# Three float32r matmuls over split operands become one plain float32 matmul

## The chip, the core and the metric

The kernel runs on one core of a Trainium2 chip. The metric is device time in microseconds (us), the median of three runs. Engines are named as the profile names them: PE is TensorE (matmuls), PEld its loads of stationary operands, DVE is VectorE, ACT ScalarE, POOL GpSimd, SP the engine that issues transfers.

## What is computed

Two layers of a hybrid block on 256 context tokens and 1024 latent tokens, width 1024, all in float32. Each layer normalises its input, modulates it, multiplies it by a wide input projection, runs four groups of heads (latent attention, global attention, windowed attention with sinks, a two-way state-space scan), and puts the gated results through one output projection with a residual.

```
h = rmsnorm(x, norm_w) * (1 + scale[:, None]) + shift[:, None]
hc = rmsnorm(xc, norm_w) * (1 + scale_c) + shift_c
pl = split_cols(h @ w_in, IN_WIDTHS)
pc = split_cols(hc @ w_in, IN_WIDTHS)
...
x = x + gate[:, None] * (jnp.concatenate([ya_l, yb_l, yc_l, yd_l], axis=-1) @ w_out)
if need_ctx_out:
    xc = xc + gate_c * (jnp.concatenate([ya_c, yb_c, yc_c, yd_c], axis=-1) @ w_out)
```

The second layer needs no context output, so its output projection covers the 8 latent tiles of 128 tokens, the first layer's all 10.

## The kernel before

**Products.** A number is kept as a pair: its rounding to float32r (hi) and the rest (lo). `mm3` (lines 127 to 130) makes a product of three matmuls, hi by hi, lo by hi and hi by lo, into one PSUM bank. It serves the input projection (`products` at line 618, 128 weight columns by up to 512 tokens, and the token-major part at line 1011, 128 tokens by 256 columns), the up-projections of the latent attention (lines 853 to 892) and the output projection (line 1377). Each contracts 1024 features in 8 steps of 128, the up-projections 128 or 256.

**Splitting.** `split_w` (line 284) loads weights into the ring `bg`, has ACT round them into one slot and DVE or POOL subtract into a second. `make_ht` (line 385) does the same with the modulated input, `third` (line 773) with queries and keys, `prep` of the output projection (line 1349) with the attention outputs. The normalised latent vectors go to DRAM as pairs (`d_c`, line 825) and come back for the up-projections (line 842).

**Attention.** For each pair of heads and each group of 512 or 256 queries, `main` (line 1196) goes over blocks of 128 keys: scores of both heads (lines 1214 to 1222), exponentials on ACT, and then, one block late, the products of probabilities and values (line 1230), which are plain float32 matmuls: the two heads write the two halves of the PSUM partitions. Row maxima of later queries are found meanwhile (`maxima`, line 1127, single float32r matmuls, DVE reduces them); minus the maximum enters the scores through one further row of the operands. In the latent branch the scores are three matmuls; in the other two branches, whose heads have 64 features, hi and lo stand on top of each other in 128 rows, and two matmuls do (lines 1219 and 1222).

**Scan.** `chunk_a` (line 522) sums decays over tokens with a triangular matrix of ones; its moving operand is split as well, so four matmuls (line 540).

**Order.** The work is written down in one order, in which scan steps, up-projections, maxima and the loads of the next weights are spread between the products of the input projection and between the blocks of attention; each engine then keeps its own queue in the order in which its instructions come out. Slots of 4 KB per partition (35 of them) are handed out and returned in program order, PSUM is divided by tags (`MX` 3 banks, `S2` 3, `ACC` 1, `TR` 2). Weight chunks are fetched one ahead of their use.

## Time and profile before

| | |
|---|---|
| median of 3 runs | 1937.92 us (1937.03 to 1938.29) |
| span of the profiled execution | 1922.1 us |
| PE busy | 1839.9 us, 9658 records |
| weight loads busy | 1327.6 us |
| DVE, ACT, POOL busy | 1128.8, 751.5, 772.8 us |
| moved by DMA | 231.52 MB |

The profile is of one execution; the span goes from its first instruction to its last. A record is what the hardware ran: a matmul of the program can leave one or two. Matmuls overlap, since the next starts while the last one drains, so the sum or the mean of their times is more than what they occupy; the distance between two starts says that. A few per cent of the records can be missing. The stages in time are roughly: preparation to 50 us, first input projection with the scan to 555, first attention to 910, first output projection to 1050, then the same for the second layer to 1460, 1810 and the end.

### The profile page before, as it was taken

The numbers are of one execution on the slowest core, as the hardware profiler recorded it, in microseconds if no ns is written. First come the engines' busy times: TensorE is split into PE (matmuls) and PEld (weight loads), VectorE is DVE, ScalarE is ACT, GpSimd is POOL, SyncE is SP. The second block draws the span as 40 slices with busy tenths as digits, with TensorE's granted clock in tenths as the row PEclk, the third lists the DMA queues.
The fourth block names the chain that finished last, engine by engine and source line by source line (L and its number), as shares of the span: only waits on it lengthen the run. The fifth ranks groups of instructions, "written<-read, shape, count | busy, mean of one in ns | idle before, by whom it ended". The sixth has DMA issues, their size and how long they took to land. (4 is left out here: it accounts for less than half of the span.)

```text
span 1922.1 us, 27855 instructions
## 1 busy us (share of the span) xinstructions
PE 1839.9 (96%) x9658; PEld 1327.6 (69%) x9658; DVE 1128.8 (59%) x2290; ACT 751.5 (39%) x2060; POOL 772.8 (40%) x735
## 2 busy tenths in 40 slices
PE   6999999999999999999999999999999999999898
PEld 4767888899854455555787778878986445555586
DVE  6867864464365555447546678745645456444854
ACT  5423433332314445445423333333321444544541
POOL 1313541143316666545223125522241566654522
PEclk9999999999999999999899999999999999999899
DMA  8464323265763233122511433232766422310421
GB/s 293 136 225 143 121 83 126 92 195 174 213 175 88 76 98 76 50 61 91 175 57 39 149 112 128 92 116 81 253 200 189 121 81 80 80 36 10 135 115 55
DMA packets 130396, 231.52 MB, mean 120 GB/s; under 512 B 13784, under 2 KB 74560, under 8 KB 130256
## 3 DMA queue, kind: packets, MB, share of 16 engines
q1 hardware_dynamic: 130256, 229.75, 38.1%
q8 instruction: 76, 1.25, 0.3%
q14 instruction: 64, 0.52, 0.1%
HBM read 161.15 MB, written 68.44 MB: 119 GB/s over the span
## 5 line engine op out<-in xcount | busy, mean ns | idle before, releaser
L1146 DVE TENSOR_REDUCE mp<-ps_s 128x1 f32<-128x512 f32 (+3 forms) x428 | 267.3, 659 | 246.3 <-PE ps_s L1142 206.8
L1242 POOL TENSOR_TENSOR ac<-ac,P 128x512 f32<-128x512 f32 (+3 forms) x248 | 301.2, 1226 | 212.9 <-ACT P L1223 185.2
L1223 ACT ACTIVATE P<-ps_st 128x512 f32<-128x512 f32 (+3 forms) x456 | 239.7, 553 | 269.7 <-PE ps_st L1222 127.7
L128 PE MATMUL ps_fm<-hh,wfm_hi 128*128 128x512 f32 x576 | 237.7, 413 | 2.8 <-DVE kb L658 2.1
L130 PE MATMUL ps_fm<-hl,wfm_hi 128*128 128x512 f32 x576 | 232.0, 403 | 2.6 <-POOL hl L403 2.3
L129 PE MATMUL ps_fm<-hh,wfm_lo 128*128 128x512 f32 x576 | 231.6, 402 | 0.0
L128 PE MATMUL ps_tm<-wtm_hi,hh 128*128 128x256 f32 x512 | 146.6, 286 | 0.9 <-DVE qkhl L783 0.9
L129 PE MATMUL ps_tm<-wtm_hi,hl 128*128 128x256 f32 x512 | 145.6, 284 | 0.0
L130 PE MATMUL ps_tm<-wtm_lo,hh 128*128 128x256 f32 x512 | 145.3, 284 | 0.0
L128 PEld LDWEIGHTS ps_fm<-hh,wfm_hi 128*128 128x128 f32 x576 | 110.0, 191 | 32.2 <-issue 8.7
L130 PEld LDWEIGHTS ps_fm<-hl,wfm_hi 128*128 128x128 f32 x576 | 110.0, 191 | 28.7 <-POOL hl L403 5.3
L1236 POOL TENSOR_TENSOR ac<-P 128x1024 f32<-128x1024 f32 (+1 forms) x30 | 65.5, 2184 | 143.5 <-ACT P L1223 138.8
L129 PEld LDWEIGHTS ps_fm<-hh,wfm_lo 128*128 128x128 f32 x576 | 109.9, 191 | 18.8 <-issue 1.1
L128 PE MATMUL ps_o<-wo_hi,yh 128*128 128x512 f32 x288 | 113.9, 396 | 0.4 <-ACT yh L1353 0.4
L129 PE MATMUL ps_o<-wo_hi,yl 128*128 128x512 f32 x288 | 113.2, 393 | 0.1
L130 PE MATMUL ps_o<-wo_lo,yh 128*128 128x512 f32 x288 | 112.9, 392 | 0.0
L1230 PE MATMUL ps_acc<-P,vt 128*64 128x512 f32 (+3 forms) x416 | 101.4, 540 | 0.5 <-ACT P L1223 0.5
L128 PEld LDWEIGHTS ps_tm<-wtm_hi,hh 128*128 128x128 f32 x512 | 98.2, 192 | 2.9 <-DVE qkhl L783 1.2
L130 PEld LDWEIGHTS ps_tm<-wtm_lo,hh 128*128 128x128 f32 x512 | 98.3, 192 | 0.8 <-issue 0.4
L129 PEld LDWEIGHTS ps_tm<-wtm_hi,hl 128*128 128x128 f32 x512 | 98.3, 192 | 0.4
L1380 POOL TENSOR_TENSOR xres<-xres,dl 128x512 f32<-128x512 f32 x32 | 41.8, 1305 | 112.3 <-DVE dl L1379 112.3
L1219 PE MATMUL ps_st<-qq,kk 128*128 128x512 f32 (+3 forms) x208 | 84.1, 404 | 0.0
(345 smaller groups left out, 4169.7 us busy)
## 6 DMA issues: line engine op xcount, KB each, us to landing
wfm_raw<-in_w_fm_dram SPq DMA_DIRECT2D x36, 512.0 KB
wm<-in_w_mod_dram SPq DMA_DIRECT2D x64, 256.0 KB
d_q<-qkhl SPq DMA_DIRECT2D x18, 512.0 KB
wm<-in_w_mod_dram SPq DMA_DIRECT2D x16, 512.0 KB
d_gate<-th SPq DMA_DIRECT2D x32, 256.0 KB
wtm_raw<-in_w_tm_dram SPq DMA_DIRECT2D x16, 512.0 KB
qq<-d_q SPq DMA_DIRECT2D x32, 256.0 KB
wo_raw<-in_w_out_dram SPq DMA_DIRECT2D x16, 512.0 KB
```

The source lines that it names most:

```text
L128: mm(o, lhsT=lh, rhs=rh, start=first, stop=False)
L129: mm(o, lhsT=ll, rhs=rh, start=False, stop=False)
L130: return mm(o, lhsT=lh, rhs=rl, start=False, stop=last)
L1146: nc.vector.tensor_reduce(out=dst, in_=p[:, :nu * w].rearrange("p (u k) -> p u k", u=nu), axis=AX.X, op=ALU.max)
L1219: mm(st, lhsT=k(k0, 128), rhs=q(q0, 128), start=True, stop=False)
L1223: nc.scalar.activation(out=pts[:, h, :w], in_=st, func=AF.Exp, scale=op["scale"])
L1230: mm(acc[h * 64:h * 64 + 64, c0:c0 + w], lhsT=op["v"].tile(kb)[:, v0:v0 + 64], rhs=pts[:, h, :w], start=(bi == 0), stop=(bi == len(blocks) ...
L1236: nc.gpsimd.tensor_tensor(out=s[:, :, :n], in0=sums[0][:, :, :n], in1=pts[:, :, :n], op=ALU.add)
L1242: eng.tensor_tensor(out=s[:, h, c0:c0 + w], in0=s[:, h, c0:c0 + w], in1=pts[:, h, :w], op=ALU.add)
L1380: (nc.vector if t == ts[-1] else nc.gpsimd).tensor_tensor(out=xt.t[:, js], in0=xt.t[:, js], in1=d, op=ALU.add)
```

## The change

`mm3` becomes `mm1`, one matmul on float32 operands. All pairs are gone: weights land in a slot directly (`load_w`), the modulated input is written once, queries, keys and up-projected operands are kept once in DRAM, the normalised latent vectors stay in SBUF. The scores of every branch are one matmul over `kd + 1` rows (97 or 65). The decay sums take two matmuls, one per direction, over unsplit operands. The maxima stay float32r and read the float32 operands under that type; in the two branches with 64 features they read one row more, which holds zeros then. Comments and docstrings are dropped.

```diff
-    def mm3(o, lh, ll, rh, rl, first, last):
-        mm(o, lhsT=lh, rhs=rh, start=first, stop=False)
-        mm(o, lhsT=ll, rhs=rh, start=False, stop=False)
-        return mm(o, lhsT=lh, rhs=rl, start=False, stop=last)
+    def mm1(o, l, r, first, last):
+        return mm(o, lhsT=l, rhs=r, start=first, stop=last)
...
-    def split_w(src, name, n=1024, eng=None):
-        raw = bg((P, n), name=name + "_raw")
-        nc.sync.dma_start(out=raw, in_=src)
-        hi = Slot([P, n], F32R, name + "_hi")
-        lo = Slot([P, n], F32R, name + "_lo")
-        nc.scalar.copy(hi.t, raw)
-        (eng or nc.vector).tensor_tensor(out=lo.t, in0=raw, in1=f32(hi.t), op=ALU.subtract)
-        return hi, lo
...
+    def load_w(src, name):
+        w = Slot([P, 1024], F32, name)
+        nc.sync.dma_start(out=w.t, in_=src)
+        return w
...
-                nc.scalar.activation(out=hf[:, :n], in_=src, func=AF.Identity, scale=sc, bias=bi)
-            hi = hh[k](lo, n)
-            nc.vector.tensor_copy(hi, hf[:, :n])
-            eng = nc.gpsimd if k % 2 else nc.vector
-            eng.tensor_tensor(out=hl[k](lo, n), in0=hf[:, :n], in1=f32(hi), op=ALU.subtract)
+                nc.scalar.activation(out=h[k](lo, n), in_=src, func=AF.Identity, scale=sc, bias=bi)
...
                 for d in range(2):
-                    for e in range(2):
-                        mm(pseg[:, 0:256], lhsT=st_r[d], rhs=ta[:, d, e, :], start=(d == 0 and e == 0), stop=(d == 1 and e == 1))
+                    mm(pseg[:, 0:256], lhsT=st_f[d], rhs=ta[:, d, :], start=d == 0, stop=d == 1)
...
-            r = mm3(p, hi.t[:, c], lo_.t[:, c], hh[k](lo, n), hl[k](lo, n), k == 0, k == 7)
+            r = mm1(p, w[0].t[:, k * P:(k + 1) * P], h[k](lo, n), k == 0, k == 7)
...
-                mm3(p[:, :n], wh, wl, *W["ck", lo], True, True)
...
+                mm1(p[:, :n], W["k"].t[:, pair * P:pair * P + P], res["ckv"](lo, n), True, True)
...
-                    if br == 0:
-                        k0, k1 = op["k"][h]
-                        mm(st, lhsT=k(k0, 96), rhs=q(q0, 96), start=True, stop=False)
-                        mm(st, lhsT=k(k1, 96), rhs=q(q0, 96), start=False, stop=False)
-                        mm(st, lhsT=k(k0, 97), rhs=q(q1, 97), start=False, stop=True)
-                    else:
-                        k0, k1 = op["k"][0]
-                        mm(st, lhsT=k(k0, 128), rhs=q(q0, 128), start=True, stop=False)
-                        if mo is not None:
-                            mm(st, lhsT=ident_r, rhs=mask_r[:, mo:mo + w], start=False, stop=False)
-                        mm(st, lhsT=k(k1, 65), rhs=q(q1, 65), start=False, stop=True)
+                    mm(st, lhsT=op["k"][h].tile(kb, 0, kd + 1), rhs=op["q"][h](lo + c0, w, 0, kd + 1), start=True, stop=mo is None)
+                    if mo is not None:
+                        mm(st, lhsT=ident_r, rhs=mask_r[:, mo:mo + w], start=False, stop=True)
...
-                    mm3(p, yh[:, k, :], yl[:, k, :], wo[k][0].t[:, js], wo[k][1].t[:, js], k == 0, k == 7)
+                    mm1(p, y[k].tile(t), wo[k].t[:, js], k == 0, k == 7)
```

Two places show how the order of PE's instructions moves. The first is in the input projection of the first layer, where scan steps (`ps_y`, `ps_yt`, `ps_seg`, `ps_cb`) stand between the products (`ps_fm`). PE before:

```order
L128 MATMUL ps_fm<-hh_441,wfm_hi 128x512
L129 MATMUL ps_fm<-hh_441,wfm_lo 128x512
L558 MATMUL ps_y<-ssd_cx,EW 128x64 x2
L561 MATMUL ps_y<-st_cx,ssd_cx 128x128 x2
L578 MATMUL ps_yt<-con,yy 128x128
L540 MATMUL ps_seg<-TA,mask_r 128x256 x2
L130 MATMUL ps_fm<-hl_446,wfm_hi 128x512
L128 MATMUL ps_fm<-hh_442,wfm_hi 128x512
L129 MATMUL ps_fm<-hh_442,wfm_lo 128x512
L130 MATMUL ps_fm<-hl_447,wfm_hi 128x512
```

PE in the changed kernel, at the like place:

```order
L125 MATMUL ps_fm<-h_544,wfm 128x512
L125 MATMUL ps_fm<-h_545,wfm 128x512
L125 MATMUL ps_fm<-h_546,wfm 128x512
L536 MATMUL ps_y<-xt,EW 128x64 x2
L539 MATMUL ps_y<-st,cf 128x128 x2
L518 MATMUL ps_seg<-TA,mask_r 128x256
L525 MATMUL ps_cb<-cf,bf 128x128
L518 MATMUL ps_seg<-TA,mask_r 128x256
L556 MATMUL ps_yt<-con,yy 128x128
L125 MATMUL ps_fm<-h_428,wfm 128x512
```

Each product is one instruction in place of three, and the scan's steps, which are as many as before, stand between whole products.

The second place is in the global attention of the first layer (`ps_st` scores, `ps_acc` values, `ps_s` maxima, `ps_m` their transpose). PE before:

```order
L1142 MATMUL ps_s<-kk_cx 128x256 x4
L1219 MATMUL ps_st<-qq_5595,kk 128x512
L1222 MATMUL ps_st<-ql_5597,k_5594 128x512
L1219 MATMUL ps_st<-qq_5596,kk 128x512
L1222 MATMUL ps_st<-ql_5598,k_5594 128x512
L1230 MATMUL ps_acc<-P,vt 64x512 x2
L1219 MATMUL ps_st<-qq_5595,kk 128x512
```

PE in the changed kernel:

```order
L1062 MATMUL ps_s<-k_cx 128x256 x4
L1129 MATMUL ps_st<-q_3664,k 128x512
L1129 MATMUL ps_st<-q_3665,k 128x512
L1090 MATMUL ps_m<-con,mt 4x128
L1139 MATMUL ps_acc<-P,vt 64x512 x2
L1129 MATMUL ps_st<-q_3664,k 128x512
```

Two score matmuls per key block stand where four stood; the maxima and the values keep their number and their place.

## Rows read from the trace of the kernel before

**Rows 1.** The page, its line of busy time: share of the span, instructions.

```profile
PE 1839.9 (96%) x9658; PEld 1327.6 (69%) x9658; DVE 1128.8 (59%) x2290; ACT 751.5 (39%) x2060; POOL 772.8 (40%) x735
```

**Rows 2.** By stage: length, busy PE, PEld, DVE, ACT, POOL, PEclk, DMA, GB/s.

```profile
0.00:50.00 50.00, 33.14 (x209) 22.97 (x209) 31.18 (x81) 27.78 (x69) 10.26 (x18) 0.93 0.84 287
50.00:555.00 505.00, 484.99 (x3107) 409.69 (x3107) 309.09 (x688) 165.95 (x411) 159.93 (x189) 0.99 0.47 152
555.00:910.00 355.00, 351.53 (x1504) 186.80 (x1503) 198.05 (x341) 171.68 (x509) 201.78 (x156) 0.98 0.30 82
910.00:1050.00 140.00, 135.54 (x617) 108.81 (x617) 76.61 (x170) 54.70 (x178) 42.69 (x38) 0.96 0.28 97
1050.00:1460.00 410.00, 390.22 (x2396) 340.27 (x2395) 259.47 (x556) 142.21 (x342) 139.64 (x165) 0.98 0.44 143
1460.00:1810.00 350.00, 344.43 (x1388) 180.10 (x1388) 193.69 (x324) 152.62 (x415) 187.94 (x141) 0.98 0.30 81
1810.00:1922.10 112.10, 100.00 (x447) 78.96 (x443) 60.71 (x136) 36.52 (x140) 30.55 (x29) 0.96 0.26 95
```

**Rows 3.** The chain that ended last, in second attention: start us, us, piece.

```profile
1512.92 1.01 PE ps_acc L1230 x4
1513.93 0.43 PE ps_s L1142
1514.36 0.43 PE ps_st L1219
1514.79 0.23 PE ps_st L1222
...
1518.86 1.87 PE ps_acc L1230 x8
```

**Rows 4.** Timeline of PE, first output projection: start us, us, instruction.

```profile
964.83 0.39 PE L128 MATMUL ps_o<-wo_hi,yh 128*128 128x512 f32 x1
...
966.19 0.39 PE L128 MATMUL ps_o<-wo_hi,yh 128*128 128x512 f32 x1
```

**Rows 5.** Timeline of PE, second input projection.

```profile
1359.74 0.28 PE L130 MATMUL ps_tm<-wtm_lo,hh 128*128 128x256 f32 x1
...
1361.18 0.28 PE L130 MATMUL ps_tm<-wtm_lo,hh 128*128 128x256 f32 x1
```

**Rows 6.** Timeline of PE, scan steps within the first input projection.

```profile
223.16 0.66 PE L561 MATMUL ps_y<-st,cf 128*128 128x128 f32 x4
223.66 0.27 PE L578 MATMUL ps_yt<-con,yy 128*128 128x128 f32 x1
```

**Rows 7.** Groups of PE instructions, shapes apart: count, busy us, mean ns, idle before.

```profile
L128 PE MATMUL ps_fm<-hh,wfm_hi 128*128 128x512 f32 x576 | 237.7, 413 | 2.8 <-DVE kb L658 2.1 <-ACT hf L399 0.3 <-DVE hh L401 0.2
...
L128 PE MATMUL ps_tm<-wtm_hi,hh 128*128 128x256 f32 x512 | 146.6, 286 | 0.9 <-DVE qkhl L783 0.9
...
L128 PE MATMUL ps_o<-wo_hi,yh 128*128 128x512 f32 x288 | 113.9, 396 | 0.4 <-ACT yh L1353 0.4
...
L1219 PE MATMUL ps_st<-qq,kk 128*128 128x512 f32 x128 | 57.6, 450 | 0.0
L128 PE MATMUL ps_fm<-hh_cx,wfm_hi 128*128 128x256 f32 x192 | 56.9, 296 | 0.0
...
L1214 PE MATMUL ps_st<-qh,kh 96*128 96x512 f32 x128 | 52.0, 406 | 0.1
...
L128 PE MATMUL ps_tm<-wtm_hi,hh_cx 128*128 128x256 f32 x96 | 28.1, 293 | 2.2 <-DVE rb L732 2.2
...
L540 PE MATMUL ps_seg<-TA,mask_r 128*128 128x256 f32 x144 | 27.5, 302 | 2.0 <-DVE TA L518 1.7
L1219 PE MATMUL ps_st<-qq,kk_cx 128*128 128x512 f32 x64 | 27.2, 445 | 0.3 <-DVE th L668 0.3
...
L1214 PE MATMUL ps_st<-qh,kh_cx 96*128 96x512 f32 x32 | 13.5, 422 | 0.0
```

**Rows 8.** Groups of PE instructions, shapes together, score line 1219.

```profile
L1219 PE MATMUL ps_st<-qq,kk 128*128 128x512 f32 (+3 forms) x208 | 84.1, 404 | 0.0
```

More of the change, by code (lines that the diff above doesn't have):

```diff
@@ L361, in alloc_ht @@
     def alloc_ht(half):
-        hh, s1 = toks([f"hh{4 * half + k}" for k in range(4)], F32R)
-        hl, s2 = toks([f"hl{4 * half + k}" for k in range(4)], F32R)
-        return hh, hl, s1 + s2
+        return toks([f"h{4 * half + k}" for k in range(4)], F32)
     def transposed(xs, lo, n, k):
@@ L613, in fetch @@
             br, half = j[1]
-            return [split_w(w_tm[L, br, half, :, u, :], f"wtm{u}", eng=nc.gpsimd if (br * 2 + half, u) in POOL_TM else None)
-                    for u in range(2)]
-        return [split_w(w_fm[L, j[1]], "wfm", eng=nc.gpsimd if j[1] in POOL_FM else None)]
+            return [load_w(w_tm[L, br, half, :, u, :], f"wtm{u}") for u in range(2)]
+        return [load_w(w_fm[L, j[1]], "wfm")]
     def products(ht, w, lo, n, tag="MX", each=lambda: None, ks=range(8), p=None):
-        hh, hl, _ = ht
-        hi, lo_ = w[0]
+        h = ht[0]
         if p is None:
@@ L814, in start_ssd, with norm @@
                 todo.extend(ssd.steps(g))
-        def norm(keys, nfeat, groups, col, c0, done):
+        def norm(keys, nfeat, groups, col, done):
             srcs = [res[k] for k in keys]
@@ L955, in in_proj @@
         conv_fin(jobs[1][3], xp, True)
-        for u in both[0] + both[1]:
-            free_all(u)
+        free_all(both[0] + both[1])
         for ji, j in enumerate(jobs):
@@ L1042, in ones_row @@
             for lo, n in ((0, NCTX), (NCTX, NLAT)):
-                nc.vector.tensor_copy(tok(lo, n, row, row + 1), ones[row:row + 1, 0:1].to_broadcast([1, n]))
+                nc.vector.tensor_copy(f32r(tok(lo, n, row, row + 1)), ones[row:row + 1, 0:1].to_broadcast([1, n]))
         def rows(tok, p0, src, with_ctx=True):
@@ L1101, in begin @@
[L1101 to L1119 removed]
+                (k, op["gate"], *qs), s0 = toks(["k", "gate", "q0", "q1"], F32)
@@ new lines, in begin @@
+                op["free"] += s0
+                op["k"], op["q"] = [k, k], qs
+                for h in range(2):
+                    rows(qs[h], 0, d_q[br - 1][h * 64:h * 64 + 64, pair, :], need_ctx)
+                    for lo, n in ((0, NCTX), (NCTX, NLAT))[0 if need_ctx else 1:]:
+                        nc.vector.tensor_copy(f32r(qs[h](lo, n, 64, 65)), tri_u[64:65, 0:1].to_broadcast([1, n]))
+                rows(k, 0, d_k[br - 1][pair * 64:pair * 64 + 64, :])
+                ones_row(k, 64)
@@ L1120, in values @@
+            def values():
+                if pair == 0:
+                    (state["vt"],), state["late"] = toks(["vt"], F32)
+                    dv = d_v[br - 1].rearrange("(t p) c -> p t c", p=P)
+                    for dst, src in ((state["vt"].cx, dv[:, 0:2, :]), (state["vt"].lat, dv[:, 2:, :])):
+                        nc.sync.dma_start(out=dst.rearrange("p (t c) -> p t c", c=P), in_=src)
+                else:
+                    op["free"] += state["late"]
                 op["v"] = state["vt"]
@@ L1329, in attention @@
                 if i + 1 == len(pairs):
-                    pieces = pieces + sum((late() for _ in range(N_LATE)), [])
+                    pieces = pieces + [late] * N_LATE
                 tail = main(op, gi, pieces, tail)
@@ L1350, in prep @@
             c = slice(t * P, (t + 1) * P)
-            yh, yl = bg((P, 8, P), F32R, name="yh"), bg((P, 8, P), F32R, name="yl")
-            for k in range(8):
-                nc.scalar.copy(yh[:, k, :], y[k].tile(t))
-                nc.vector.tensor_tensor(out=yl[:, k, :], in0=y[k].tile(t), in1=f32(yh[:, k, :]), op=ALU.subtract)
-            if t == NTILE - 1:
-                free_all([u for u in y_slots if not need_ctx or u.t.shape[1] == NLAT])
             xt = Slot([P, DM], F32, "xres")
@@ L1399, in out_proj @@
                 xt.free()
-        for w in wo:
-            free_all(w)
-        free_all([u for u in y_slots if need_ctx and u.t.shape[1] != NLAT])
+        free_all(wo + y_slots)
         if last:
@@ L1487, in late @@
         def late():
[L1489 to L1503 removed]
+            if len(wo) < 8 and len(free_slots) >= 1:
+                wo.append(load_w(w_out[L, len(wo)], "wo"))
         def follow(res):
```

225 lines of the change are left out of this document (66 added, 159 removed).

## The prediction

> **What bounds the kernel now.** I read the busy line first: TensorE (PE) is busy 96% of the span, its weight loads 69%, VectorE 59%, ScalarE 39%, GpSimd 40% [rows 1]. Matmuls are pipelined, so 96% does not yet say that PE is full; the table by stage [rows 2] says where it is not. PE is idle by that table for 17 us in the first 50, 20 in the first input projection, 4 in the first attention, 4 in the first output projection, 20 in the second input projection, 6 and 12 in the last two stages: 82 us in all. The reader is to see that no other engine comes near: VectorE reaches its highest share, about 62%, in the first 50 us and in the two input projections. PE has further gaps that a busy share hides: in the chain of attention [rows 3] a matmul that opens a group takes 0.43 us, the next ones 0.23 or 0.24, so a wait at the head of a group costs some 0.2 us even where no idle time is shown. PE is the bound in every stage but the first, so the change is priced by PE's own time, and everything it frees elsewhere is worth only what it takes out of those gaps.
>
> **What one product costs, before and after.** Before, a product of 512 columns is three single-pass matmuls, and they start every 0.227 us: seven starts in a row span 1.36 us, 966.19 less 964.83, six steps [rows 4]. So 0.68 us per product. With 256 columns twelve steps take 1.44 us, 0.120 each, 0.36 per product [rows 5].
>
> After, it is one plain float32 matmul. The kernel before has such matmuls too: the product of probabilities and values (line 1230). Two heads make two matmuls of the program, and the chain shows four records for them, so the hardware makes two records of each plain matmul. One such step of four records takes 1.01 us, two steps in a row, eight records, take 1.87 us [rows 3]: the second adds 0.86 us, and since the two heads run side by side in the two halves of the array, 0.86 us is what one plain matmul of 512 columns occupies, 0.43 a record. That is twice the single-pass rate, so a record streams its columns twice and the product four times. I take 0.86 us at 512 columns, and by width 0.44 at 256 (0.43 plus a little, because the weights are loaded twice).
>
> No row shows a plain matmul over the whole width of the array with that many columns; the nearest at full width has 128 columns, four records from 223.16 until the transpose that follows starts at 223.66, some 0.12 each [rows 6]. That bounds the record from both sides. If the 0.12 is only the load of its weights, the columns themselves could go through once, 0.23 us at 512 columns and 0.45 a product. If the load of the second record were not hidden behind the first, a record would take 0.505 (half of the 1.01 us, in which one load and one wait are exposed), 1.01 a product. I take 0.43, from the row with the same number of columns.
>
> The Trainium skill's page "FP8 and Floating Point Precision", section "TensorE Precision Notes", says that true FP32 takes four passes through the array (high and low halves crossed). The chain's 0.86 us against 4 times 0.227 agrees for half-width matmuls; by the page the full-width ones, which no row here shows, cost the same, and the sum stays as below. Against it stands the page "TensorE: Matmul & The Clock Gate", section "Back-to-back issue gap", which gives about 131 ns per matmul of 512 columns as the sustained rate with its loads. By that a third more passes would add only 0.13 us a product, and the largest term below would be 139 us instead of 192. The trace disagrees, 0.227 us each in a stretch that nothing interrupts, and I follow the trace.
>
> **The sum, part by part.** Counts are those of the first of the three matmuls [rows 7], where a plain product will stand.
> - Products of three, 512 columns: 576 of the input projection, 288 of the output projection, 128 and 32 scores of the latent attention, and 40 in the up-projections (by the code's loops): 1064, each 0.86 less 0.68, so 0.18: +192 us.
> - Products of three, 256 columns: 192 of the context, 512 and 96 token-major ones, 40 small ones by the code: 840 times (0.44 less 0.36): +67 us.
> - Scores of the other two branches. Here three products stood packed in two matmuls, 128 rows deep and 65 rows deep, so two passes become four: 128 and 64 of them with 512 columns, each 0.86 less 0.45, so 0.41: +78 us. The 80 narrower ones against latent keys (208 less 128 [rows 8]) and 16 of the context, by their width some 0.2 each where they gain anything: +16 us.
> - The decay sums of the scan (line 540): 144 single-pass matmuls in 36 places become two plain ones each, 0.88 less 0.48: +14 us.
> - The maxima (line 1142) stay single-pass, the transposes and the value products are untouched: 0.
>
> That is +367 us on PE's path. All of it lies on the path, since in the stages where it falls PE waits little.
>
> **What is freed.** Rounded copies on ScalarE and subtractions on VectorE and GpSimd go (weights, inputs, latent vectors, queries, keys, the output projection's operands), and so does the way of the latent vectors through DRAM. All these ran beside PE, so most of it is worth nothing. What can come back: of the 82 us idle the first 50 us hold 17, in which transfers and the normalisation of x decide (DMA at 0.84 of its capacity [rows 2]), and the last stage 12, of which the tail behind the last matmul is a part: neither moves. Of the other 53, part is PE waiting for pieces that VectorE makes late, with 62% of its time taken; I count half, 27. PE's granted clock is 0.93 to 0.99 of full in the seven stages, 0.98 weighted by their length [rows 2], so some 2% of the span's clock is lost (up to 40 us) to times at the lower of its two levels, 1.2 GHz; the lowest stands in the stage that is idle for the largest share, and fewer gaps may return a third, 13 us. Together 40, with 0 and about 110 as ends (nothing; or all 53, all of the clock's cost and a bit of the hidden waits). The waits at the heads of groups stay, because the groups stay.
>
> A wait could move: the weights now land directly in the buffers that the products read, without a staging ring. They are fetched one chunk ahead, and with half as many halves alive the buffers turn over more slowly, so I see no new wait and count 0; if that cover failed, a load of 128 x 1024 float32 (512 KB) would stand in front of its products, 1.8 us at the 287 GB/s of the first 50 us [rows 2], and 52 such loads by the code would cost 95 us at worst.
>
> The profiled execution has a span of 1922.1 us; the median of the timed runs is 15.8 us above it, which I take as what lies around the span. 1922 + 367 - 40 + 16 = 2265 us, 17% slower.
>
> By stage: the first output projection has 160 products, so +29 us on its 140, the second +23; each attention +60 or a little more on its 350; the input projections, first and second, some +100 and +90 on 505 and 410, less what is recovered.
>
> **Rivals.**
> - *One pass per record (faster than before).* Place: every full-width plain matmul. If a record costs 0.23 us at 512 columns, the product takes 0.45 instead of 0.68: 1064 times -0.23, 840 times about -0.12, scores unchanged, so about -345 us and a time near 1600 us, where the shorter path would meet VectorE and give some back, say 1650. It decides from 0.34 us a record, where three passes and two records are equal. For it: full-width rows with 128 columns would look the same if loading decides. Against: 0.43 at the same number of columns in half the width, and no reason why the width should change how often columns are streamed. Chance 4%.
> - *Loads not hidden (far slower).* 0.505 us a record: +0.33 on 1064, +0.145 on 840, +0.56 on 192, and 40 for the rest, 620 us, so about 2520. For it: the 1.01 us of a step on its own. Against: the 0.12 us records with 128 columns, each with its own load of 128 columns, which leave no room for a load that is not overlapped. 5%.
> - *Much more comes back.* If the split work was what made PE late in the input projections and at the edges of stages, and all 110 return: 2195. For it: the idle rows of both input projections. Against: within attention, where a third of the increase lies, no split runs. 13%.
> - *Nothing comes back.* The order changes, waits stay where they are, and longer matmuls hold back the pieces of the scan: 2305, up to 2345 with the worse end of the weight waits in part. 18%.
>
> **How the numbers follow.** Forecast 60%, the rivals 4, 5, 13 and 18. The forecast's own range is 2235 to 2295. For 8 in 10 I reach to the recovered and the unrecovered case: 2190 to 2345; the two ends of the unknown record cost (1650, 2520) stay outside with 9% between them. A measurement tells about 0.2% of this kernel's time, 4 us. Slower 0.95, same 0.01, faster 0.04.
>
> **What would show it.** Lines for plain products with twice the program's count of records, starting about 0.43 us apart at 512 columns and 0.22 at 256; output projections near 169 and 135 us long; PE still above 95% busy, VectorE well under half. I am wrong if the starts are 0.23 or 0.5 us apart, or if the idle time of PE grows in the input projections.

## The result, and the profile after

The changed kernel takes 2164.84 us (median of 4 runs, 2162.17 to 2167.4) against 1938.06 us of the kernel before on the same chip: 1.117 times as long, 95% interval 1.115 to 1.118. The prediction was 2265 us (2190 to 2345): the direction is right, the rise is 227 us where 327 were forecast, and the time lies below the range.

The page's line of busy time, after:

```profile
PE 2125.0 (98%) x7754; PEld 1152.7 (53%) x7754; DVE 901.2 (42%) x1862; ACT 628.8 (29%) x1732; POOL 671.5 (31%) x679
```

Beside [rows 1]: PE rises by 285 us, VectorE falls by 228, ScalarE by 123, GpSimd by 101. The other engines lost work, PE gained some, and PE is still the bound.

The table by stage, after (columns as in [rows 2]); the stages are cut here from their first to their last matmul: input projection, attention, output projection, and the same of the second layer.

```profile
36.40:611.90 575.50, 574.64 (x2405) 371.51 (x2404) 249.39 (x594) 125.39 (x332) 117.63 (x163) 1.00 0.36 116
611.90:1024.20 412.30, 410.15 (x1439) 181.39 (x1438) 189.08 (x322) 182.50 (x525) 203.35 (x159) 0.93 0.17 52
1024.20:1162.30 138.10, 137.85 (x328) 61.05 (x327) 26.32 (x53) 17.91 (x63) 28.40 (x28) 1.00 0.22 77
1168.80:1659.80 491.00, 487.61 (x1858) 308.28 (x1857) 220.07 (x493) 101.00 (x269) 104.07 (x144) 1.00 0.30 95
1659.80:2040.10 380.30, 377.75 (x1281) 161.98 (x1279) 164.92 (x286) 162.86 (x435) 188.13 (x147) 0.93 0.15 47
2040.10:2152.00 111.90, 110.75 (x265) 49.31 (x265) 26.26 (x48) 13.73 (x48) 23.15 (x23) 1.00 0.10 36
```

Two things stand out against [rows 2]. The input projections, where PE was idle for some 20 us each, are full (0.9 and 3.4 us idle). And the granted clock of both attentions is 0.93, lower than in any of these stages before, though PE is idle there for only 2 to 3 us.

The timeline of PE in the output projection, after (start, length, instruction, records):

```profile
1049.41 1.88 PE L125 MATMUL ps_o<-wo,y 128*128 128x512 f32 x4
1051.13 1.88 PE L125 MATMUL ps_o<-wo,yd 128*128 128x512 f32 x4
```

Four records every 1.72 us, 0.43 each at full width: the price read from the half-width matmuls of [rows 3] holds. The groups of [rows 7] now stand with twice the program's count:

```profile
L125 PE MATMUL ps_fm<-h,wfm 128*128 128x512 f32 x1152 | 523.8, 593 | 0.2 <-ACT xcc L651 0.2
L125 PE MATMUL ps_tm<-wtm,h 128*128 128x256 f32 x1024 | 228.9, 379 | 0.0
```

To separate work from waiting I give every PE instruction the step at which its kind follows itself when nothing holds it (0.227 and 0.120 us for single-pass matmuls of 512 and 256 columns, 0.429 and 0.215 for a record of a plain one) and add up. This estimate of PE's needed work is about 1610 us before and 1970 us after, +360 (the prediction's sum was +367). What a stage takes beyond it is called its waits below; time lost at the lower clock counts among them. The price was right; the waits were not. The chain of the second attention, after, shows where [rows 3] changed beside the scores themselves (start us, us, piece):

```profile
1743.55 0.89 PE ps_s L1062 x3
1744.44 1.72 PE ps_st L1129 x4
1746.16 1.01 PE ps_acc L1139 x4
1747.17 0.66 PE ps_s L1062 x2
```

In [rows 3] the first matmul of a maximum (`ps_s`) behind the value products took 0.43 us, and the first score behind the maximum 0.43 again. Here the former stays (0.89 for three, 0.43 + 2 x 0.23), and the scores behind it, four records, take 1.72 = 4 x 0.43 with nothing on top.

Stage lengths in us of the profiled execution of each kernel, first to last matmul (in, att, out: input projection, attention, output projection, of layers 1 and 2), and the median time (ratio to the kernel before, run on the same chip). Input and output projections that an edit does not touch agree within 3 us between runs, so their lengths are compared across the table. Attentions differ more, by the time that the clock was low in them: the first one of the kernel before is 362.3 us long, the same instructions in the run with plain output projections take 376.6. The kernel before had a median of 1923 to 1925 us in the later measurements (executions of its slower state left out), and its clock and time move together from run to run (1937 us at a mean clock of 0.972, 1918 at 0.983).

| kernel | in 1 | att 1 | out 1 | in 2 | att 2 | out 2 | time, ratio |
|---|---|---|---|---|---|---|---|
| before | 520.2 | 362.3 | 112.7 | 444.7 | 340.8 | 89.2 | 1938 |
| after | 575.5 | 412.3 | 138.1 | 491.0 | 380.4 | 111.8 | 2165, 1.117 |
| after, narrower products | 499.6 | 382.1 | 138.1 | 420.5 | 386.8 | 111.9 | 2019, 1.045 |
| before, plain products, splits kept | 592.1 | 363.7 | 140.8 | 504.8 | 337.1 | 111.4 | 2106, 1.094 |
| before, plain output projections | 518.0 | 376.6 | 140.9 | 447.0 | 343.0 | 111.7 | 1980, 1.028 |
| after, rows filled | 575.4 | 387.8 | 138.1 | 492.8 | 356.1 | 111.9 | 2116, 1.098 |
| after, burst | 575.6 | 388.3 | 138.1 | 492.7 | 361.7 | 111.8 | 2123, 1.105 |
| rows filled, scores two-pass | 575.8 | 344.6 | 138.1 | 489.9 | 321.4 | 111.9 | 2041, 1.060 |
| rows filled, maxima of 64 rows | 583.1 | 409.4 | 138.1 | 498.4 | 373.2 | 111.8 | 2168, 1.126 |
| before, rows filled | 517.5 | 336.2 | 110.5 | 441.4 | 316.3 | 89.2 | 1863, 0.969 |
| before, maxima of 128 rows | 509.7 | 338.0 | 110.5 | 436.6 | 320.8 | 89.2 | 1859, 0.965 |

### The profile page after: what moved, and what is told of

Same layout as the page of the kernel before. It is cut to its first block, busy times and chain, and to the rows that moved or that the text cites. A ratio compares the mean times of both kernels' runs of the same rounds, so it can differ in the third digit from the quotient of the medians.

```text
span 2160.4 us, 22669 instructions
## 1 busy us (share of the span) xinstructions
PE 2125.0 (98%) x7754; PEld 1152.7 (53%) x7754; DVE 901.2 (42%) x1862; ACT 628.8 (29%) x1732; POOL 671.5 (31%) x679
## 4 chain that ended last, share of the span: by engine, by line
PE 94%; DVE 2%; DMA 1%; issue 1%; POOL 1%; ACT 0%; SPq 0%; DVEq 0%; POOLq 0%; ACTq 0%
PE ps_fm L125 26%; PE ps_st L1129 18%; PE ps_tm L125 11%; PE ps_o L125 11%; PE ps_acc L1139 10%; PE ps_s L1062 5%; PE ps_seg L518 2%; PE ps_q L125 1%; PE ps_sum L1185 1%; DMA x<-in_x_dram 1%; PE ps_y L539 1%; PE ps_state L482 1%; PE ps_moda L238 1%; PE ps_y L536 1%; PE ps_xt L355 1%
## 5 line engine op out<-in xcount | busy, mean ns | idle before, releaser
L125 PE MATMUL ps_fm<-h,wfm 128*128 128x512 f32 x1152 | 523.8, 593 | 0.2 <-ACT xcc L651 0.2
L1129 PE MATMUL ps_st<-q,k 65*128 65x512 f32 (+4 forms) x672 | 321.5, 594 | 0.0
L125 PEld LDWEIGHTS ps_fm<-h,wfm 128*128 128x128 f32 x1152 | 208.4, 190 | 206.6 <-issue 201.0
L125 PE MATMUL ps_tm<-wtm,h 128*128 128x256 f32 x1024 | 228.9, 379 | 0.0
L125 PEld LDWEIGHTS ps_tm<-wtm,h 128*128 128x128 f32 x1024 | 192.6, 190 | 31.8 <-issue 6.5
L1129 PEld LDWEIGHTS ps_st<-q,k 65*128 65x128 f32 (+1 forms) x672 | 127.9, 202 | 102.9 <-issue 87.3
L125 PE MATMUL ps_o<-wo,y 128*128 128x512 f32 x384 | 170.7, 593 | 0.0
L1062 PE MATMUL ps_s<-k,q 65*128 65x512 f32 (+3 forms) x320 | 131.2, 475 | 1.4 <-DVE mp L1066 1.3
L1129 PE MATMUL ps_st<-q,k_cx 65*128 65x512 f32 (+1 forms) x192 | 95.6, 631 | 1.3 <-DMA q<-ng 1.3
L125 PE MATMUL ps_fm<-h_cx,wfm 128*128 128x256 f32 x384 | 93.3, 382 | 0.0
```

The lines of the kernel that those rows point to most:

```text
L125: return mm(o, lhsT=l, rhs=r, start=first, stop=last)
L1062: mm(o, lhsT=f32r(qh(lo + t * P, P, 0, km)), rhs=f32r(kh(k0, w, 0, km)), start=True, stop=mo is None)
L1129: mm(st, lhsT=op["k"][h].tile(kb, 0, kd + 1), rhs=op["q"][h](lo + c0, w, 0, kd + 1), start=True, stop=mo is None)
```

## The experiments

**Where the waits of the input projections went.** Two runs fill the square between before and after: one has the helpers' work of after with PE's time of before, the other the reverse.

```
--- after
+++ e1_narrow
-            r = mm1(p, w[0].t[:, k * P:(k + 1) * P], h[k](lo, n), k == 0, k == 7)
+            c = n if k == 0 else {512: 392, 256: 208}[n]
+            r = mm1(p[:, :c], w[0].t[:, k * P:(k + 1) * P], h[k](lo, n)[:, :c], k == 0, k == 7)
... (the same for the token-major products)
--- before, in mm3
+++ e2_keep_split
... (the three matmuls go)
+        odd[0] ^= 1
+        l, r = (ll, rl) if odd[0] else (lh, rh)
+        return mm(o, lhsT=l.bitcast(F32), rhs=r.bitcast(F32), start=first, stop=last)
```

> The changed kernel, but of the eight products of each group of the input projections the second to the eighth take 392 of their 512 columns (208 of 256), so that a group of plain float32 products occupies TensorE about as long as the 24 float32r matmuls of the kernel before (8 x 0.68 us). The products of the columns left out are missing from the result. No splitting is put back. In the kernel before TensorE waited 54 us in the first input projections and 47 us in the second beside its needed work; in the changed kernel 13 and 9. Theory A (the splitting on ScalarE, VectorE and GpSimd made TensorE wait, and it is gone): the waits stay near 13 and 9 us, the input projections lose some 85 and 80 us, the time is about 2000 us. Theory B (nothing was freed; the longer matmuls only cover the other engines' pieces): the waits come back to about 50 and 45 us, the time is about 2075 us.

> The kernel before with all its splitting, but each product of the input projections, up-projections and output projections is one plain float32 matmul, of the first halves and of the second halves in turn (so TensorE still depends on both; the other terms of the product are missing). Scores and segments are as before. By the prices read from the traces TensorE has 904 products x 0.18 us and some 820 narrow ones x 0.07 us more to do, about 218 us. Theory A (the splitting made TensorE wait): the waits of the input projections stay near 54 and 47 us, and the time is about 1938 + 218 = 2155 us. Theory B (longer matmuls cover the pieces of the other engines, splitting or not): the waits fall toward 13 and 9 us, and the time is about 2075 us.

The first took 2018.68 us (1.045, interval 1.037 to 1.053), the second 2105.99 us (1.094, 1.088 to 1.099). Their input projections by stage (columns as in [rows 2]), first those of the kernel before, then of the run with narrower products, then of the one that keeps the splits:

```profile
37.50:557.70 520.20, 500.12 (x3210) 419.87 (x3206) 321.60 (x715) 172.58 (x422) 163.54 (x192) 0.99 0.48 153
...
1039.30:1484.00 444.70, 423.99 (x2521) 360.59 (x2522) 286.81 (x596) 150.78 (x355) 146.15 (x170) 0.98 0.44 142
```

```profile
37.80:537.30 499.50, 495.46 (x2404) 361.77 (x2403) 249.97 (x594) 125.22 (x331) 118.60 (x163) 1.00 0.42 133
1064.10:1484.50 420.40, 414.26 (x1858) 300.11 (x1857) 218.03 (x491) 101.23 (x269) 105.57 (x144) 1.00 0.34 110
```

```profile
38.10:630.20 592.10, 576.65 (x2397) 366.15 (x2396) 322.79 (x712) 172.60 (x422) 163.74 (x192) 1.00 0.44 138
1141.60:1646.40 504.80, 493.55 (x1866) 304.83 (x1866) 285.91 (x601) 150.59 (x355) 143.27 (x170) 0.99 0.42 132
```

Waits beyond the needed work, first and second layer:

| | PE's time of before | PE's time of after |
|---|---|---|
| splits kept | 54 + 47 = 101 (before) | 37 + 28 = 65 |
| splits gone | 20 + 12 = 32 | 13 + 9 = 22 (after) |

(The run that keeps the splits keeps the single-pass decay sums too, so PE needs 8 and 6 us less in its input projections than in those of the changed kernel.) Removing the splits, with all that goes with them, takes away 69 of the 79 us; longer matmuls alone take away 36, and the times say the same: 218 us were priced for them and 182 came (2106 against 1924). 13 us of the upper row belong to the maxima, below; without them it is 88 and 52, and the shares are 56 and 36 of 66. Neither theory has it alone. The two overlap, which fits a PE that waits wherever the other engines' pieces for a group take longer than its own, whichever side of that comparison moves; no run here shows it piece by piece. The removed splitting was worth PE time, then, though no other engine came near its limit.

**Whether the price stands alone.** The output projections hardly waited before, so they show it bare.

```
--- before
+++ e7_out_plain
-                    mm3(p, yh[:, k, :], yl[:, k, :], wo[k][0].t[:, js], wo[k][1].t[:, js], k == 0, k == 7)
+                    yk, wk = (yl, wo[k][1]) if k % 2 else (yh, wo[k][0])
+                    mm(p, lhsT=f32(yk[:, k, :]), rhs=f32(wk.t[:, js]), start=k == 0, stop=k == 7)
```

> The kernel before with only the output projections changed: each product is one plain float32 matmul, of the first halves at even and of the second halves at odd blocks of features (the other terms are missing), all splitting as before. TensorE waited only 4 and 2 us in these two stages, so the price of a product stands alone here: 288 products x (0.858 - 0.681) = 51 us. Theory P (the price per record is right and only the waits were misjudged): the stages go from 113 and 89 us to about 140 and 111, the time rises by 48 to 51 us. Theory Q (the price was too high too): they rise by clearly less, the time by under 40 us.

The stages went from 112.7 and 89.2 to 140.9 and 111.7 us, +50.7 together: theory P, to a microsecond. The time rose by 55 us (1979.81 against 1924.8; 1.028, 1.024 to 1.033), somewhat more than the stages; in the profiled execution the first attention, which the edit leaves alone, is 14 us longer, at a lower clock (below).

**The clock of the attentions.** In the trace after, the first global attention begins like this, by stretches of 1 and 10 us (the last columns are granted clock, DMA share, GB/s):

```profile
617.00:618.00 1.00, 1.00 (x3) 0.48 (x2) 0.08 (x1) 0.33 (x1) 0.00 (x0) 0.50 0.89 282
...
620.00:630.00 10.00, 10.00 (x17) 2.73 (x16) 1.00 (x2) 2.12 (x4) 3.60 (x2) 0.50 0.06 18
...
670.00:680.00 10.00, 10.00 (x17) 3.15 (x18) 0.00 (x0) 2.60 (x5) 3.79 (x3) 0.58 0.00 0
680.00:690.00 10.00, 10.00 (x40) 4.34 (x38) 4.53 (x8) 6.11 (x23) 4.25 (x3) 1.00 0.00 0
```

PE is busy in all of it, at 1.2 GHz for 61 us, with 17 records in 10 us. The second layer has the same for 51 us. What came ahead, in PE's timeline:

```profile
612.84 0.63 PE L1062 MATMUL ps_s<-k,q 65*128 65x512 f32 x2
614.75 1.09 PE L1062 MATMUL ps_s<-k,q 65*128 65x512 f32 x2 [1.27 <-DVE mp L1066]
615.68 5.72 PE L1129 MATMUL ps_st<-q,k_cx 65*128 65x512 f32 x8
```

PE stood still for 1.27 us, then came maxima and scores over 65 rows, and the clock fell at 617, 1.3 us into the scores. At half speed for 61 and 51 us, PE lost some 56 us in the two layers.

```
--- after
+++ e3_pad_rows
+                for tok in [k] + qs:
+                    for lo, n in ((0, NCTX), (NCTX, NLAT))[0 if need_ctx or tok is k else 1:]:
+                        nc.gpsimd.memset(tok(lo, n, 64, P), 0.0)
...
+                    kr = P if br else kd + 1
+                    mm(st, lhsT=op["k"][h].tile(kb, 0, kr), rhs=op["q"][h](lo + c0, w, 0, kr), start=True, stop=mo is None)
--- after
+++ e4_burst
+            if br == 1 and op["pair"] == 0 and gi == 1:
+                burst = ps("S2", name="ps_burst")
+                for i in range(32):
+                    mm(burst, lhsT=ident_r, rhs=mask_r[:, 0:512], start=i == 0, stop=i == 31)
```

> The changed kernel, but the score matmuls of the two grouped-query branches contract over 128 rows instead of 65, the further rows of both operands filled with zeros by GpSimd (12 fills a layer pair at most, beside the loads). The matmuls' columns are the same, so TensorE's needed work is the same. In the changed kernel the granted clock was 0.50 for 61 us and 51 us from the first scores of the global attention on, some 59 us of lost time. Theory R (the few rows in use keep the clock at the lower level): the two stretches shrink to those of the kernel before (7 and 10 us), the time is about 2110 us. Theory W (the wait of 1.3 us ahead of the attention and plain float32 as such decide): the stretches stay, the time is 2165 us within 5.

> The changed kernel with 32 float32r matmuls of 128 rows and 512 columns (the identity by the masks, into a bank that nobody reads) ahead of the first scores of the global attention in both layers: 32 x 0.227 = 7.3 us each at full clock, part of them in a wait of 1.3 us that is there. Theory W (the clock falls because TensorE stood still just before): the burst bridges the wait, the two stretches at 0.50 (61 and 51 us) shrink to a few us or vanish, the time is about 2165 - 59 + 12 = 2118 us. Theory R (the scores over 65 rows pull the clock down whatever went before): the stretches begin some 7 us later and last as long, the time is about 2178 us.

2115.96 us with filled rows (1.098, 1.092 to 1.105) and 2123.13 with the burst (1.105, 1.097 to 1.113). The same place with filled rows, in the timeline and by stretches:

```profile
615.13 1.10 PE L1065 MATMUL ps_s<-k,q 65*128 65x512 f32 x2 [1.28 <-DVE mp L1069]
616.07 3.60 PE L1133 MATMUL ps_st<-q,k_cx 128*128 128x512 f32 x8
```

```profile
620.00:630.00 10.00, 10.00 (x34) 3.86 (x32) 4.73 (x8) 3.39 (x7) 6.12 (x4) 1.00 0.07 23
```

And with the burst:

```profile
620.00:630.00 10.00, 10.00 (x35) 4.67 (x33) 4.47 (x7) 3.58 (x6) 2.38 (x2) 1.00 0.20 57
```

With filled rows the wait is still there, 1.28 us, and the clock stays up; with the burst the scores still have 65 rows, and it stays up too. In this kernel either edit ends the stretch, then. The filled rows give back 24 us in each attention, 49 in all, the burst 24 and 19 net of its own time. One of the burst's four runs is 25 us longer than the others (2148 us, mean clock 0.984 against 0.996), as one such stretch would make it; it has no profile.

A rule does not follow, for other traces show the parts one by one. In the run with narrower products the first global attention begins with a wait of 0.80 us and scores over 65 rows, and the clock stays up:

```profile
540.14 3.67 PE L1131 MATMUL ps_st<-q,k_cx 65*128 65x512 f32 x8 [0.80 <-DVE mp L1068]
```

```profile
540.00:550.00 10.00, 9.86 (x27) 3.75 (x27) 4.97 (x9) 3.99 (x7) 3.62 (x2) 1.00 0.68 177
1490.00:1500.00 10.00, 10.00 (x14) 3.22 (x14) 2.03 (x4) 2.39 (x4) 2.34 (x1) 0.50 0.41 128
```

The second of these rows is its second global attention, behind a wait of 1.44 us: 61 us at 0.50. In the run with maxima of 64 rows (below) the scores have 128 rows, the wait is 1.28 us again, and the clock falls all the same, for 7 us:

```profile
627.00:628.00 1.00, 1.00 (x2) 0.56 (x3) 1.00 (x3) 0.00 (x0) 0.00 (x0) 0.50 1.02 239
...
634.00:635.00 1.00, 1.00 (x5) 0.20 (x4) 0.00 (x0) 0.60 (x1) 0.09 (x1) 1.00 0.00 0
```

And in the kernel before it fell at 563 us with no wait at all: PE is busy throughout, with maxima over 64 rows among scores over 128 and 65.

```profile
555.00:560.00 5.00, 5.00 (x21) 3.02 (x19) 3.60 (x7) 0.83 (x2) 0.00 (x0) 1.00 0.38 116
560.00:565.00 5.00, 5.00 (x13) 2.02 (x14) 4.37 (x8) 2.28 (x4) 0.72 (x1) 0.81 0.61 177
```

That stretch lasted 7 us. With the same instructions at that place it lasted 34 us in the run with plain output projections and 38 in the one with bursts in the kernel before (below), and the run that keeps the splits has none there. So plain float32 is no condition either. What the profiles have in common is this: every stretch of more than 14 us stood at the start of a global attention that has scores over 65 rows, and where those scores had 128 rows none of more than 7 us did. From the run with plain output projections:

```profile
565.00:570.00 5.00, 5.00 (x11) 1.74 (x9) 0.69 (x1) 1.19 (x2) 2.50 (x3) 0.50 1.05 225
...
595.00:600.00 5.00, 5.00 (x21) 2.04 (x21) 1.76 (x4) 2.44 (x5) 2.70 (x3) 1.00 0.00 1
```

One such stretch in place of two is also what would put the profiled run with narrower products (1993.83 us) 25 us under its other three (2018 to 2021), whose mean clock was 0.966 to 0.969 against 0.982.

**The attentions.** With the clock mended they are 25 and 15 us longer than before, where the price of their products says 65 and 60. Some 40 us of waits came back in each. The attentions before and with filled rows:

```profile
557.70:920.00 362.30, 356.18 (x1529) 189.34 (x1527) 202.24 (x345) 178.08 (x537) 206.45 (x159) 0.97 0.31 85
...
1484.00:1824.80 340.80, 332.03 (x1369) 174.01 (x1368) 188.96 (x314) 159.65 (x441) 196.04 (x148) 0.97 0.28 77
```

```profile
612.30:1000.20 387.90, 382.88 (x1440) 173.46 (x1438) 181.92 (x322) 182.75 (x525) 211.65 (x171) 1.00 0.18 55
1637.60:1993.60 356.00, 353.63 (x1281) 155.15 (x1279) 163.26 (x286) 162.81 (x435) 196.91 (x155) 1.00 0.16 50
```

The first guess was the splitting again.

```
--- e3_pad_rows
+++ e6_scores_two_pass, branches 1 and 2
+                        mm(st, lhsT=f32r(op["k"][h].tile(kb, 0, P)), rhs=f32r(op["q"][h](lo + c0, w, 0, P)), start=True, stop=False)
...
+                        mm(st, lhsT=f32r(op["k"][h].tile(kb, 0, 65)), rhs=f32r(op["q"][h](lo + c0, w, 0, 65)), start=False, stop=True)
...
```

> The changed kernel with the rows filled to 128 (as in the run with filled rows), but the scores of the two grouped-query branches are again two float32r matmuls, over 128 and over 65 rows as in the kernel before, both on the same unsplit operands and with the scale halved (so the scores are only float32r products). The loads and copies of the second halves stay gone. By the prices read, TensorE has 192 x 0.41 + about 8 = 86 us less to do than with one plain float32 matmul. With filled rows the two attentions took 388 and 356 us, against 362 and 341 before, though their plain matmuls need 65 and 60 us more, so some 40 us of waits came back in each. Theory A (the missing split operands gave them back): they stay back, the attentions take about 345 and 315 us, the time is about 2116 - 86 = 2030 us. Theory B (the longer score matmuls covered what TensorE waits for): the shorter matmuls bring the waits again, the attentions take about 375 and 345 us or more, the time is 2085 to 2105 us.

2041.43 us (1.060, 1.056 to 1.065), the attentions 344.6 and 321.4: close to theory A's numbers. The difference to one plain matmul, 43.3 and 34.7 us, is 78 in all. That is the prediction's term for the 192 wide scores alone; by the steps in the traces the 96 narrow ones are worth another 20 us (an estimate), so some 20 us of waits came back with the shorter matmuls, as theory B has it, on a smaller scale. And most of what theory A puts down to the splitting had another reason, as the last runs show.

**Looking for a faster kernel.** Two edits of the kernel before, meant for its clock.

```
--- before
+++ e5_before_burst
+                if br == 2 and op["pair"] == 1 and gi > 0 and h == 0:
+                    burst = ps("MX", name="ps_burst")
+                    for i in range(10):
+                        mm(burst, lhsT=ident_r, rhs=mask_r[:, 0:512], start=i == 0, stop=i == 9)
--- before
+++ e8_before_rows
...
+                        nc.gpsimd.memset(f32(tok(lo, n, 64, P)), 0.0)
...
-                        mm(st, lhsT=k(k1, 65), rhs=q(q1, 65), start=False, stop=True)
+                        mm(st, lhsT=k(k1, P), rhs=q(q1, P), start=False, stop=True)
...
+                    km = P if br else kd
+                    mm(o, lhsT=qh(lo + t * P, P, 0, km), rhs=kh(k0, w, 0, km), start=True, stop=mo is None)
```

> The kernel before with four bursts of ten dense float32r matmuls (identity by masks, into a bank that nobody reads, 2.3 us each) ahead of the sums of the last two groups of queries of each layer, where TensorE waited 2.3 to 4.5 us for VectorE and the granted clock then was 0.50 for 27 us in all. If standing still there is what costs the clock, the bursts take up waits that are there and the clock stays up: up to 27/2 = 13 us less than the kernel before, a ratio of about 0.993. If the waits are not where the clock is decided, or the bursts only delay what follows: 0 to 9 us more, 1.000 to 1.005.

> The kernel before, with the score matmuls of the two grouped-query branches that contracted over 64 or 65 rows (lines 1142 and 1222) contracting over 128: the further rows of the third pass are filled with zeros by GpSimd, and the maxima read the second halves that stand in the same tile. The number of matmuls and their columns are the same. In the profiles of the kernel before and of two that share its attention, the granted clock was 0.50 at the start of the first global attention for 7, 34 and 38 us and for 10 to 14 us at the start of the second. Theory R (few rows in use let the clock fall there): these stretches go, 6 to 20 us less than the kernel before, a ratio of 0.990 to 0.997. Theory N (filled rows help only the plain float32 scores): no difference beyond 2 us, a ratio of 0.999 to 1.001.

The bursts gave nothing (1.0035, 1.0005 to 1.0065, within the 0 to 9 us more of the second case): in their profile the clock was low for 17 us at those places instead of 27, worth 5 us, and the forty matmuls of the bursts take 9, not all of it within the waits. The filled rows gave 1863.21 us, 0.969 (0.964 to 0.973), three times the most that was expected. The clock accounts for little of it: time at the lower level fell from 81 to 54 us, worth 14. So something else about the rows is dear, and the trace of before has it, where maxima stand among the products of the last input projection:

```profile
548.35 0.40 PE L130 MATMUL ps_fm<-hl,wfm_hi 128*128 128x512 f32 x1
548.67 0.49 PE L1142 MATMUL ps_s<-kk,qq 64*128 64x512 f32 x1
549.10 0.50 PE L128 MATMUL ps_fm<-hh,wfm_hi 128*128 128x512 f32 x1
549.43 0.40 PE L129 MATMUL ps_fm<-hh,wfm_lo 128*128 128x512 f32 x1
549.67 0.40 PE L130 MATMUL ps_fm<-hl,wfm_hi 128*128 128x512 f32 x1
550.00 0.49 PE L1142 MATMUL ps_s<-kk,qq 64*128 64x512 f32 x1
```

All are single-pass with 512 columns. The step onto the matmul of 64 rows is 0.32 us, the step off it 0.43, the one behind 0.33; four of them, to the next `ps_s` at 550.00, take 1.33 us where 0.91 would do (4 x 0.227). One visit to 64 rows costs 0.42 us here. The change did away with these visits in passing: its maxima contract over 65 rows. Two runs for that, one from each side.

```
--- e3_pad_rows
+++ e9_max64
-            km = kd if br == 0 else kd + 1
+            km = kd
--- before
+++ e10_before_max128
-                    mm(o, lhsT=qh(lo + t * P, P, 0, kd), rhs=kh(k0, w, 0, kd), start=True, stop=mo is None)
+                    km = P if br else kd
+                    mm(o, lhsT=qh(lo + t * P, P, 0, km), rhs=kh(k0, w, 0, km), start=True, stop=mo is None)
```

> The changed kernel with the rows of the scores filled to 128, but the matmuls of the maxima in the grouped-query branches (line 1062) contract over 64 rows, as in the kernel before, and not over 65, as the change has made them. In the trace of the kernel before a 512-column float32r matmul is followed after 0.23 us by one with as many rows, and after 0.32 to 0.42 us where one of the two has 64 rows and the other more; there are 360 such neighbours in its input projections and attentions. Theory S (the change of rows between 64 and more costs TensorE about 0.11 us each time, and the change took it away by the way, with its 65 rows): 360 x 0.11 = 40 us more than with 65 rows, the attentions take about 405 and 372 us instead of 388 and 356, the time is about 2156 us. Theory A (the missing split operands alone gave the waits of the attentions back): no difference, 2116 us within 4.

> The kernel before with one line changed: the matmuls of the maxima in the grouped-query branches (line 1142) contract over the 128 rows of the same tile instead of its first 64; the third pass of the scores stays at 65 rows, and nothing is filled. Theory S (the change of rows between 64 and more costs 0.11 us each time): 360 x 0.11 = 40 us less, the time is about 1885 us, the attentions take about 342 and 322 us instead of 362 and 341. Theory F (what made the kernel before 61 us faster with filled rows was the third pass and the clock): no more than 5 us less, about 1920 us.

64 rows put into the changed kernel: 2168.27 us (1.126, 1.123 to 1.130), 52 more than with 65. 128 rows put into the kernel before: 1858.67 us, 0.965 (0.962 to 0.969), 65 less. That is theory S with a higher price than expected: 52 us where 40 stood, and of the 65 about 12 go with less time at the lower clock (57 us of it in the profile against 81), which leaves much the same. Over the 180 visits (360 neighbours) 52 us are 0.29 each, so the 0.42 of the place above is more than the average. The attentions of the two, first with 64 rows in the changed kernel, then with 128 in the kernel before:

```profile
623.20:1032.60 409.40, 405.04 (x1439) 174.76 (x1437) 183.14 (x322) 182.84 (x524) 211.26 (x171) 0.99 0.17 52
1675.70:2048.90 373.20, 371.55 (x1281) 155.81 (x1279) 165.09 (x286) 162.84 (x435) 196.72 (x155) 1.00 0.14 47
```

```profile
547.00:885.00 338.00, 329.28 (x1528) 188.16 (x1526) 207.36 (x347) 177.50 (x536) 208.58 (x159) 0.98 0.34 93
...
1438.70:1759.60 320.90, 311.15 (x1370) 173.43 (x1369) 191.78 (x315) 159.06 (x441) 198.01 (x148) 0.98 0.30 82
```

And the same sort of place as above in the latter, every step 0.22 to 0.23:

```profile
540.21 0.39 PE L1143 MATMUL ps_s<-kk,qq 128*128 128x512 f32 x1
540.43 0.39 PE L129 MATMUL ps_fm<-hh,wfm_lo 128*128 128x512 f32 x1
540.66 0.39 PE L130 MATMUL ps_fm<-hl,wfm_hi 128*128 128x512 f32 x1
540.89 0.39 PE L1143 MATMUL ps_s<-kk,qq 128*128 128x512 f32 x1
```

With all its splitting the kernel before then has attentions of 338.0 and 320.8 us, against 344.6 and 321.4 of the run with unsplit operands and two passes. PE has some 14 us less to do in each of them (an estimate: the latent scores, three single passes against a plain matmul), so its waits are some 8 and 13 us longer, of which about 4 and 6 are the lower clock (10 and 16 us of it against 3 and 3). Some 11 us are left as the most that the splitting can have cost both attentions together, so theory A of that run falls as the main cause. This one line makes the fastest kernel of the study, 3.5% under the kernel before and 13 to 14% under the changed one.

The Trainium skill's page "TensorEngine Tiling (Array Packing)", section "Tiling Modes", says that the array can work as two tiles of 64 rows each, and that changing the tiling mode drains TensorE. The trace agrees as far as it goes: 64 rows beside 128 cost 0.42 us a visit, 65 or 96 beside 128 cost nothing (0.235 us a step). No run here shows in which mode the array worked.

## Why the prediction was wrong

The balance of the two profiled spans, 2160.4 - 1922.1 = +238 us:

| term | predicted | measured | from |
|---|---|---|---|
| PE's needed work | +367 | +360 | starts and counts of both traces |
| waits of the input projections | part of -40 | -66 | 101 to 22, less 13 of the next row |
| visits to 64 rows | 0 | -52 | 64 against 65 rows, filled kernel |
| lower clock at the start of the global attention | part of -40 | +49 | after against filled rows (56 by half the stretches) |
| other waits of the attentions | part of -40 | -45 | 39 and 45 come back, less 22 and 17 of the visits |
| output projections, ends | 0 | -8 | remainder |

- **What one product costs**: right. 0.429 us a record at full width, 0.215 at 256 columns, two records a matmul; the rivals of 0.23 and 0.505 fall. Output projections +25 and +23 us where +29 and +23 stood; the scores of two branches 78 us, net of some 20 us of waits, where 78 and 16 stood.
- **What is freed**: the step that failed. It started from the 82 us that the table by stage shows as idle, counted half of the 53 that could move, 27, and 13 of the clock's cost, and put the waits that a busy share hides at nothing. Some 160 us came back, against 49 lost to the clock. Most of the 160 is not idle time in any row: it lies inside steps that are longer than they need be. By stage the miss is largest in the input projections, +55 and +46 us where some +100 and +90, less what is recovered, stood.
- **"The waits at the heads of groups stay, because the groups stay"**: the sentence in that step that was wrong outright. The rows it rested on, 0.43 us for `ps_s` L1142 and again for `ps_st` L1219 [rows 3], are two things: the one behind the value products stays after the change (0.89 us for three) and with maxima of 128 rows, the other, from the maximum to the scores, is the step between 64 and 128 rows and goes with it. In the chain after, no score behind a maximum has such a step.
- **"The maxima (line 1142) stay single-pass ...: 0"**: single-pass they stayed, but one row more took them out of the 64-row form, and that was worth 52 us. The change had the line, and the prediction priced its passes alone.
- **The clock**: a gain of 13 us was counted. Outside the two long stretches the time at the lower level did fall, from 81 us to 9, and that gain is part of the waits above; but the two stretches cost 49, and no row of before showed one of that size (7 us at that place in its profile).
- **What lies around the span**: 1.8 us in every run that has both numbers, not 16. The rest of the 16 lies between the profiled execution and the timed ones; by the later runs, where time and clock move together, 1938 us means a clock near 0.972, and the profile has 0.979. The spans differ by 238 us, the medians by 227.
- **New waits of weight loads**: 0, right; the first input projection has 0.9 us of idle time in all.
- **The rival "much more comes back"** (2195 us, 13%) named the right mechanism for the input projections, if not the only one. The objection to it, that no split runs within attention, is not quite true (VectorE rounds and subtracts weights of the output projection there, 12.6 us between 575 and 905) and was beside the point: most of what came back there was something else. That its 2195 us is the nearest of the prediction's numbers is luck: the terms of 52, 45 and 49 us are not in it.

What stays open: of the 45 us of other waits in the attentions about 17 are the kernel before's own time at the lower clock (38 us of it in the two attentions, 3 with filled rows, half of it lost). Of the other 28, some 20 come back when the scores are two-pass again, so the longer scores covered them; about 8 no run isolates, and the splitting may have a part in them. What lets the clock fall at the start of the global attention, and why it then stays low for 7 us in one run and 38 in another, no run settles.

## What to carry to other kernels

Price the waits of a bound engine by its steps, start to start against the best step of the same kind, and not by its idle time: here 82 us were idle and twice as much came back. Where a step is long, compare it with a step whose neighbours differ in one thing (rows, columns, type, bank) before calling it a wait; the shape of a neighbour can be the cause, and one line then outdoes a rewrite. Work on engines that are far from full can still hold the full one up piece by piece, and either shorter pieces there or longer ones here lessen that.

## What the runs showed of the hardware

- A float32r matmul of 512 columns that contracts over 64 rows, between such of 128, cost 0.42 us more than one of 65, 96 or 128 rows, by the steps around it. All such visits together cost 52 us in the changed kernel (0.29 each) and, with the clock's share taken off, about as much in the kernel before.
- TensorE can be busy without a break and stay at the lower clock: 61 and 51 us of the trace after, 17 records in 10 us instead of 34. There it began where a wait of 1.3 us was followed by scores of 65 rows; with scores of 128 rows, or without the wait, the clock stayed at 1.00 in the profiles. In the kernel before it fell with no wait, and with 128 rows in the scores and 64 in the maxima it fell after one, for 7 us each time.
- A plain float32 matmul over the full array is two records of 0.429 us at 512 columns, as long as two half-width ones take side by side.
